# Attention values' high and low parts in one 128-column matrix, padded decay products, and a planner with another matmul time

## The chip, the cores and the metric

The kernel runs on one core of a Trainium2 chip. The metric is the device time of one execution in microseconds (us); the median of three runs stands for it. Below, TensorE (PE) is the matrix engine, VectorE (DVE), ScalarE (ACT) and GpSimd (POOL) the elementwise engines, and SyncE (SP) issues most transfers. PSUM is the memory that products are accumulated in (8 banks of 512 columns here), which VectorE and ScalarE read in this kernel and GpSimd does not.

## The reference

Two model blocks run over 512 tokens of width 1024, in float32.

The first block has a short-convolution layer with a gated feed-forward layer, then an attention layer with three branches (compressed blocks, selected blocks, sliding window) over 16 heads of 64 in 4 groups that share keys and values, again with a feed-forward layer. With 512 tokens all eight selected blocks of 64 fit in the 16 that may be selected, and the window covers the whole sequence, so both branches see every earlier token:

```python
p = jax.nn.softmax(s.reshape(s.shape[:4] + (n_sel * L_SLC,)), axis=-1).reshape(s.shape)
o_slc = jnp.einsum("bghqnl,bgqnld->bqghd", p.astype(v_sel.dtype), v_sel)
...
p = jax.nn.softmax(jnp.where(m, s, NEG_INF), axis=-1)
o_win = jnp.einsum("bghqk,bkgd->bqghd", p.astype(vw.dtype), vw)
o = (gblk[..., 0:1] * o_cmp + gblk[..., 1:2] * o_slc + gblk[..., 2:3] * o_win)
```

The second block has two mixers side by side, a state-space mixer of 16 heads in chunks of 128 tokens, whose weights within a chunk are `decay = exp(where(causal, seg, -inf))`, and a stick-breaking attention of 16 heads, `outs.append(jnp.einsum("bhqk,bhkd->bhqd", weights, vp))`; then an output projection and a feed-forward layer, each scaled by a condition.

## The kernel before

Products in float32 are made of parts: an operand is split into a high part, rounded to the matrix engine's one-pass format, and the low rest (`split`, `hilo`: the high part by a copy, the low one by a subtraction). `mm3` (line 608) issues three products into one PSUM tile: high by high, high by low, low by high. Nearly every product of the kernel comes in such threes; a weight matrix arrives by transfer as `raw`, and is split into `wh` and `wl`.

The activations are held with features on the partitions and the 512 tokens as columns. Stages follow one another: layer a, a feed-forward layer, the keys and values (`nsa`, line 862), attention in 16 units (4 groups times 4 tiles of 128 queries), the output projection "o", a feed-forward layer, the second block's mixers (`block2`, line 1163), and its last layers. `weave` (line 87) interleaves the generators of a stage by fractions of their length, so projections, scores and values of different units stand side by side in the program.

Attention values, first block (`nsa_values`, line 1123): for every key tile and branch (steps: 2, 4, 6 or 8 per unit, 80 in all) four transposes write one PSUM tile "pt"; it is split into "pth" (a copy on ScalarE) and "ptl" (a subtraction on VectorE); three steps later `mm3` multiplies them with the values of that tile, 64 columns of "vh" or "vl", into 64 partitions of one PSUM tile "o". Twelve small products with the compressed values follow, and four copies of 64x128 take "o" to SBUF ("o2"). After the fourth unit of a group both tiles "o2" are split for the output projection.

Values, second block (`sb_out`, line 1559): per head, four key tiles with 512, 384, 256 and 128 query columns, each one `mm3` with 64-column values ("svh", "svl") into 64 partitions of "so", then one copy of 64x512. The values themselves come from `sb_qk` (line 1438) token-major and are split whole, 512 columns at a time.

Decay (`ssd_pair`, line 1354, function `weights`): per head one product "al" spreads a row of the 64-row tile "at" over all partitions, with a selector of 64 rows, `er`, as its matrix; the four "dec" subtractions read it.

The order of the instructions is planned, not written: `Recorder` (line 156) records every instruction, then `arrange` runs a list scheduler forward and backward over durations that `cost` (line 242) gives, and emits each engine's instructions in the planned order. Each engine executes its own in that order. Some instructions may go to one of several engines (`any`, line 195): copies to ScalarE or VectorE, and to GpSimd where both operands are in SBUF on the same partitions and have 256 columns or more; additions and subtractions to VectorE, or GpSimd under the same condition. An addition that reads PSUM has only VectorE. A product's cost is `size * passes / 2.4 + 3.0` ns (line 254), and the next may not start before its own matrix is loaded, columns / 1.2 ns (line 256). The scheduler considers instructions up to 800 places ahead of the first one that is not yet placed.

The lines of almost all instructions are one line of a helper (485), so the profile is read by tile names.

Of the kernel before, what the change touches and what calls it, by code (L numbers as in the profile page):

```python
# [6 lines left out]
F32R = mybir.dt.float32r  # L7
# [4 lines left out]
D = 1024  # L12
# [16 lines left out]
LAG = 3  # L29
# [57 lines left out]
def weave(*streams):  # L87
    """emits instruction streams side by side: (generator, the total of what it yields, start, end)"""
    live = [[float(st[2] if len(st) > 2 else 0), i, st] for i, st in enumerate(streams)]
    while live:  # L90
        s = min(live)
        g, total = s[2][:2]
        a, b = s[2][2:] if len(s[2]) > 2 else (0.0, 1.0)
        try:
            s[0] += (b - a) * next(g) / total
        except StopIteration:
            live.remove(s)
# [12 lines left out]
class View:  # L110
    """an access pattern of a tile that gets its place when the instructions are ordered"""
# [21 lines left out]
class Slot:  # L133
    """one tile as the program sees it, from its first access to its last"""
# [21 lines left out]
class Recorder:  # L156
    """records the instructions of the program, orders those of every engine by the time at which their
    operands are there and by their place in the program, and gives the tiles their places"""
# [8 lines left out]
    # from the end on one engine to the start on another  # L167
# [27 lines left out]
    def any(self, *ways):  # L195
        """one instruction that several engines can do, the usual one first: (engine, method, arguments)"""
# [45 lines left out]
    def cost(self, o, method, a, k, outs, ins):  # L242
        """nanoseconds on the engine, and those of a transfer"""
# [3 lines left out]
        # a scalar per partition  # L247
# [4 lines left out]
        elif o.eng == "tensor":  # L252
            passes = 1 if ins[-1].dtype == F32R else 2 if method == "transpose" else 6
            o.dur = size(outs[0]) * passes / 2.4 + 3.0
            # the next product waits until its own matrix is loaded
            o.load = (int(ins[0].ap.shape[-1]) if method == "matmul" else 128) / 1.2
# [13 lines left out]
    def place(self, ap):  # L270
        """the pattern on the place its tile got"""
# [23 lines left out]
    def backward(self):  # L295
        """the latest starts, from the end of the program"""
# [30 lines left out]
    def forward(self, urgent, look, timed=False):  # L327
# [26 lines left out]
        def avail(t):  # L354
            """when the tile can have a place, or None"""
# [15 lines left out]
        def begin(e, i, limit):  # L371
            """when the engine can start the instruction, or None if not by the limit"""
# [14 lines left out]
            if e in other:  # L387
                # one engine at a time reads a bank
                for t in o.banks:
                    at = max(at, t.read.get(other[e], -1e9) + self.LAG[other[e]][e])  # L390
            if e != o.eng:
                # another engine has to be done with it earlier than the usual one
# [8 lines left out]
        while first < len(ops):  # L401
            best = None
            for e, lst in cand.items():
# [10 lines left out]
                if top is not None and timed and e in self.PATIENT:  # L414
                    # a more urgent one that is ready soon goes first if that makes the later of the two less late
# [74 lines left out]
class Body:  # L490
# [26 lines left out]
    def alike(*views):  # L517
        """whether the Pool engine can do it: in SBUF, on the same partitions, of a size that is worth it"""
# [22 lines left out]
    def copy(self, out, a, scale=None):  # L541
        """a, by a factor"""
# [21 lines left out]
    def load(self, g, parts=None):  # L564
        """starts the transfer of a group of weight blocks"""
# [59 lines left out]
    def dense_g(self, name, n, x, ks=None, m=128):  # L625
        """the same as dense, in steps"""
# [7 lines left out]
    def dense_seq(self, specs, x, ks=None, first=2, late=1):  # L634
        """yields the finished PSUM tile of every (name, n); the late operands are used last in the first tiles,
        or every operand in all of them before the next one"""
# [10 lines left out]
    def dense_halves(self, specs, x, ks=None):  # L647
        """the same for the halves of the tokens, the first halves of all tiles before the second ones"""
# [12 lines left out]
    def dense_late(self, specs, x, first):  # L661
        """dense_seq where the second halves of the tokens come later: the first tiles take them last"""
        out = [self.ps("d") for _ in range(first)]
        for h, sl in enumerate(HALVES):
            for (name, n), p in zip(specs, out):
                # one accumulation group per bank: its first write clears the bank's flags
# [6 lines left out]
    def rsq(self, src, scale, eps):  # L673
        """rsqrt(scale * src + eps) by logarithm and exponential, and a step of Newton"""
# [10 lines left out]
    def allsum(self, acc):  # L685
        """the sums over the partitions, on all of them"""
# [35 lines left out]
    def setup(self):  # L722
# [18 lines left out]
        self.er = self.nc.tile([64, 16], F32R, "er")  # L741
        nc.vector.tensor_copy(self.er, self.cst[0:64, C_E:C_E + 16])
# [71 lines left out]
    def ffn(self, x, rinv, name, gate, after, ada=False, early=0, late=0):  # L814
        """early: the first tiles take the second halves of the tokens last; late: the last tiles in halves"""
# [34 lines left out]
    def dense_out(self, name, x, late, ks=None, **kw):  # L850
        """the tiles of a product with the residual's rows, the last ones in halves: (n, PSUM, columns)"""
# [10 lines left out]
    def nsa(self):  # L862
# [19 lines left out]
        def project():  # L882
            for br, n in (("s", 4), ("w", 8), ("s", 6), ("w", 10)):
                for t in range(2):
# [5 lines left out]
                    else:  # L890
                        self.vt[br, t] = self.hilo(self.transpose4(r), name="v")
# [10 lines left out]
        # gates token-major  # L902
# [50 lines left out]
    def stack(self, r, par, name="qs"):  # L953
        """[hi; lo] of one half of the rows, hi in its own rows"""
# [63 lines left out]
    def nsa_group(self, g):  # L1018
        """operands of one group of heads: stacked queries, doubled keys, distances, compressed values"""
# [103 lines left out]
    def nsa_values(self, g, qt):  # L1123
# [14 lines left out]
        for j in range(len(steps) + LAG):  # L1138
# [6 lines left out]
            if j >= LAG:  # L1145
                kt, br = steps[j - LAG]
                c = 128 * kt + 64 * (g % 2)
                v = self.vt[br, g // 2]
                self.mm3(o[0:64], (v[0][:, c:c + 64], v[1][:, c:c + 64]), x.pop(j - LAG), j == LAG, False)
            yield 1  # L1150
        for h in range(4):
            vh, vl = gr["vc"][:, 64 * h:64 * h + 64], gr["vc"][:, 256 + 64 * h:320 + 64 * h]
            self.mm3(o[0:64, h * 128:(h + 1) * 128], (vh, vl), (ph, pl), False, h == 3)
        for h in range(4):
            dst = o2[h // 2][64 * (h % 2):64 * (h % 2) + 64, qt * 128:(qt + 1) * 128]
            self.copy(dst, o[0:64, h * 128:(h + 1) * 128])
# [6 lines left out]
    def block2(self):  # L1163
        nc = self.nc
        self.cols2()
        # final norm of the first block and the first norm of the second
# [541 lines left out]
```

## Time and profile before

| what | value |
|---|---|
| median of three runs | 2162.2 us (2161.71 to 2162.23) |
| the profiled execution, first to last instruction | 2159.8 us |
| TensorE busy | 2117.5 us, 98% |
| VectorE busy | 1386.1 us, 64% |
| ScalarE busy | 941.8 us, 44% |
| GpSimd busy | 425.9 us, 20% |
| share of the chain that ended last | TensorE 86%, VectorE 9%, ScalarE 2%, issue 2%, GpSimd 1% |
| matrix products | 11113 |

The profile is of one execution, and it shows no time for it other than the span; the median of the runs is 2.4 us above that. Busy is the share of time in which an instruction of the engine is shown as running. For TensorE this says little by itself: products overlap, the end of each is modelled, and one of 512 columns is shown as about 0.39 us whatever the distance to the next. Starts are better: the distance between the starts of neighbours is what a product takes. VectorE's and ScalarE's instructions overlap by about a tenth of a microsecond in the same way. Idle time is what no instruction covers, and the engine named behind the arrow is the one whose result ended it.

### The profile page before, as it was taken

The numbers are of one execution on the slowest core, as the hardware profiler recorded it, in microseconds if no ns is written. First come the engines' busy times: TensorE is split into PE (matmuls) and PEld (weight loads), VectorE is DVE, ScalarE is ACT, GpSimd is POOL, SyncE is SP. The second block draws the span as 40 slices with busy tenths as digits, with TensorE's granted clock in tenths as the row PEclk, the third lists the DMA queues.
The fourth block names the chain that finished last, engine by engine and source line by source line (L and its number), as shares of the span: only waits on it lengthen the run. The fifth ranks groups of instructions, "written<-read, shape, count | busy, mean of one in ns | idle before, by whom it ended". The sixth has DMA issues, their size and how long they took to land.

```text
span 2159.8 us, 28829 instructions
## 1 busy us (share of the span) xinstructions
PE 2117.5 (98%) x11113; PEld 1789.1 (83%) x11113; DVE 1386.1 (64%) x2347; ACT 941.8 (44%) x1587; POOL 425.9 (20%) x558
## 2 busy tenths in 40 slices
PE   8999999999999999999999999999999998999999
PEld 7888888888788777888888887989897888888887
DVE  6578754644868996654355598787879867333333
ACT  4233322332335885322222477677667746222221
POOL 1023320211223763000000141221315222000000
PEclk9999999999999999999999999999999999999999
DMA  4245652533332000222222332111121124222222
GB/s 166 98 178 188 212 183 97 175 117 104 104 127 72 1 1 31 97 98 98 98 98 98 117 127 79 59 50 59 59 69 40 40 95 140 98 98 98 98 98 98
DMA packets 60682, 214.04 MB, mean 99 GB/s; under 512 B 7424, under 2 KB 7552, under 8 KB 60544
## 3 DMA queue, kind: packets, MB, share of 16 engines
q1 hardware_dynamic: 52704, 186.50, 24.9%
q0 software_dynamic: 7840, 25.70, 3.5%
q8 instruction: 87, 1.43, 0.3%
q14 instruction: 51, 0.42, 0.1%
HBM read 210.07 MB, written 2.10 MB: 98 GB/s over the span
## 4 chain that ended last, share of the span: by engine, by line
PE 86%; DVE 9%; ACT 2%; issue 2%; POOL 1%; DMA 0%; SPq 0%; DVEq 0%; ACTq 0%; POOLq 0%
PE d L485 71%; PE qk L485 5%; PE bt L485 2%; PE o L485 2%; DVE wl L485 1%; PE so L485 1%; PE pt L485 1%; PE s L485 1%; DVE pr L485 1%; PE lg L485 1%; DVE e L485 1%; DVE ptl L485 1%; ACT wh L485 1%; DVE ss L485 0%; PE chid L485 0%
## 5 line engine op out<-in xcount | busy, mean ns | idle before, releaser
L485 ACT CAST wh<-raw 128x1024 fp32r<-128x1024 f32 (+1 forms) x332 | 347.6, 1048 | 873.1 <-PE d L485 736.8
L485 DVE TENSOR_TENSOR wl<-raw,wh 128x1024 fp32r<-128x1024 f32 (+1 forms) x342 | 424.6, 1242 | 417.3 <-ACT wh L485 414.5
L485 PE MATMUL d<-xh,wh 128*128 128x512 f32 (+1 forms) x1064 | 417.4, 394 | 6.0 <-ACT xh L485 6.0
L485 PE MATMUL d<-xh,wl 128*128 128x512 f32 (+1 forms) x1064 | 416.5, 392 | 1.0 <-DVE wl L485 1.0
L485 PE MATMUL d<-xl,wh 128*128 128x512 f32 x1064 | 416.3, 391 | 0.0
L485 PE MATMUL d<-hb,wh 128*128 128x512 f32 (+1 forms) x1136 | 332.7, 377 | 3.6 <-ACT hb L485 3.3
L485 PEld LDWEIGHTS d<-xh,wh 128*128 128x128 f32 (+1 forms) x1064 | 200.5, 189 | 47.6 <-ACT xh L485 6.0
L485 PEld LDWEIGHTS d<-hb,wh 128*128 128x128 f32 x1136 | 205.5, 190 | 40.1 <-ACT hb L485 3.5
L485 PEld LDWEIGHTS d<-xh,wl 128*128 128x128 f32 (+1 forms) x1064 | 200.3, 188 | 43.7 <-DVE wl L485 1.8
L485 PEld LDWEIGHTS d<-xl,wh 128*128 128x128 f32 x1064 | 200.4, 188 | 41.6 <-issue 0.7
L485 PE MATMUL d<-hb,wl 128*128 128x512 f32 (+2 forms) x568 | 212.3, 376 | 2.5 <-DVE wl L485 2.5
L485 PE MATMUL d<-hidh,wl 128*128 128x512 f32 (+1 forms) x561 | 211.8, 378 | 0.0
L485 PE MATMUL d<-hidh,wh 128*128 128x512 f32 (+1 forms) x561 | 211.5, 377 | 0.0
L485 PE MATMUL d<-hidl,wh 128*128 128x512 f32 (+1 forms) x561 | 211.5, 377 | 0.0
L485 PE MATMUL qk<-wh,hb 128*128 128x256 f32 x768 | 145.0, 288 | 2.1 <-ACT hb L485 1.0
L485 POOL TENSOR_TENSOR acc<-acc,sq 128x512 f32<-128x512 f32 (+1 forms) x24 | 38.2, 1591 | 499.7 <-ACT sq L485 441.9
L485 PEld LDWEIGHTS qk<-wh,hb 128*128 128x128 f32 x768 | 121.8, 193 | 6.5 <-DVE hb L485 1.5
L485 PEld LDWEIGHTS d<-hb,wl 128*128 128x128 f32 (+1 forms) x568 | 107.3, 190 | 22.6 <-DVE wl L485 3.5
L485 PEld LDWEIGHTS d<-hidl,wh 128*128 128x128 f32 x561 | 105.6, 188 | 19.4
L485 PEld LDWEIGHTS d<-hidh,wh 128*128 128x128 f32 x561 | 105.6, 188 | 19.3
L485 PEld LDWEIGHTS d<-hidh,wl 128*128 128x128 f32 x561 | 105.6, 188 | 19.2
L485 PE MATMUL qk<-wl,hb 128*128 128x256 f32 x384 | 109.0, 286 | 1.5 <-DVE wl L485 1.5
(370 smaller groups left out, 3678.5 us busy)
## 6 DMA issues: line engine op xcount, KB each, us to landing
raw<-in_wall_dram SPq DMA_DIRECT2D x345, 512.0 KB, 3.2
ada<-in_wada_dram POOLq DMA_DIRECT2D x96, 256.0 KB, 4.6
res<-in_x_dram SPq DMA_DIRECT2D x8, 256.0 KB, 7.3
out_dram<-res SPq DMA_DIRECT2D x8, 256.0 KB, 2.0
raw<-in_wall_dram SPq DMA_DIRECT2D x2, 256.0 KB, 3.7
cond<-in_c_dram POOLq DMA_DIRECT2D x2, 256.0 KB, 5.3
cst<-in_consts_dram SPq DMA_DIRECT2D x1, 394.5 KB, 7.0
mst<-in_consts_dram SPq DMA_DIRECT2D x1, 320.0 KB, 3.8
```

Source lines behind the costliest of these rows:

```text
L485: r = getattr(getattr(self.real, o.eng), m)(*[self.place(x) for x in a], **{n: self.place(x) for n, x in k.items()})
```

## The change

Three things change together (comments and descriptions that went out with them are left out here).

- `side` lays the high and low parts of the values next to each other, 64 columns each, so that one 128-column matrix holds both. `mm2` then issues two products instead of three: the pair of value parts by the high part and by the low part of the weights. The upper 64 partitions of the PSUM tile hold what the low part of the values adds; `folded` copies them to SBUF, and an addition joins them with the lower 64. In the first block the small products with the compressed values move ahead of the last pair.
- The decay product's tile `at` and its selector `er` get 128 rows instead of 64, the added ones zero.
- The planner's cost of a product is 17/16 of a 2.4 GHz column plus 1 ns, and the load of a matrix 3 ns more.

```diff
+    COLUMN = 17 / 16 / 2.4
...
-            o.dur = size(outs[0]) * passes / 2.4 + 3.0
-            o.load = (int(ins[0].ap.shape[-1]) if method == "matmul" else 128) / 1.2
+            o.dur = size(outs[0]) * passes * self.COLUMN + 1.0
+            o.load = (int(ins[0].ap.shape[-1]) if method == "matmul" else 128) / 1.2 + 3.0
...
+    def side(self, src, name):
+        p = self.pg(F32R, name)
+        v = p.rearrange("p (a h d) -> p a h d", h=2, d=64)
+        self.split(src.rearrange("p (a d) -> p a d", d=64), v[:, :, 0], v[:, :, 1])
+        return p
+    def mm2(self, out, v, x, start, stop):
+        self.nc.tensor.matmul(out, v, x[0], start=start, stop=False)
+        self.nc.tensor.matmul(out, v, x[1], start=False, stop=stop)
+    def folded(self, p):
+        t = self.pg(name="fo")
+        self.copy(t[0:64], p[64:128])
+        return t[0:64]
...
-        self.er = self.nc.tile([64, 16], F32R, "er")
-        nc.vector.tensor_copy(self.er, self.cst[0:64, C_E:C_E + 16])
+        self.er = self.nc.tile([128, 16], F32R, "er")
+        nc.vector.tensor_copy(self.er, self.cst[:, C_E:C_E + 16])
...
-                        self.vt[br, t] = self.hilo(self.transpose4(r), name="v")
+                        p = self.transpose4(r)
+                        self.vt[br, t] = [self.side(p[:, 256 * i:256 * i + 256], "v") for i in range(2)]
...
-                self.mm3(o[0:64], (v[0][:, c:c + 64], v[1][:, c:c + 64]), x.pop(j - LAG), j == LAG, False)
+                c = 256 * (kt % 2) + 128 * (g % 2)
+                v = self.vt[br, g // 2][kt // 2][:, c:c + 128]
+                last = j == len(steps) + LAG - 1
+                if last:
+                    (the twelve products with the compressed values)
+                self.mm2(o, v, x.pop(j - LAG), j == LAG, last)
...
-            self.copy(dst, o[0:64, h * 128:(h + 1) * 128])
+            self.tt(dst, o[0:64, h * 128:(h + 1) * 128], t[:, h * 128:(h + 1) * 128], ADD)
...
-        self.at = self.pg(F32R, "at")[0:64]
+        self.at = self.pg(F32R, "at")
...
-            mm(al, self.er[:, hd:hd + 1].to_broadcast([64, 128]), self.at, start=True, stop=True)
+            mm(al, self.er[:, hd:hd + 1].to_broadcast([128, 128]), self.at, start=True, stop=True)
...
-            self.sv[i] = [self.hilo(x, name="sv") for x in p]
+            self.sv[i] = [self.side(p[t // 2][:, 256 * (t % 2):256 * (t % 2) + 256], "sv") for t in range(4)]
...
-                c = 256 * (kt % 2) + 64 * (hd % 4)
-                self.mm3(out[0:64, 128 * kt:512], [y[:, c:c + 64] for y in self.sv[2 * (hd // 4)][kt // 2]],
+                c = 128 * (hd % 4)
+                self.mm2(out[:, 128 * kt:512], self.sv[2 * (hd // 4)][kt][:, c:c + 128],
                          (hi[:, o:o + n], lo[:, o:o + n]), u == 2, u == 1)
...
-        self.copy(self.y_sb[-1][64 * h:64 * h + 64], out[0:64])
+        self.tt(self.y_sb[-1][64 * h:64 * h + 64], out[0:64], self.folded(out), ADD)
```

## Rows read from the trace of the kernel before

**Rows 1.** The page's busy times: engine, us, share of the span, instructions.

```profile
PE 2117.5 (98%) x11113; PEld 1789.1 (83%) x11113; DVE 1386.1 (64%) x2347; ACT 941.8 (44%) x1587; POOL 425.9 (20%) x558
```

**Rows 2.** Stretches: length, busy us of five engines (instructions), granted clock, DMA share, GB/s.

```profile
690.00:820.00 130.00, 123.92 (x852) 99.72 (x850) 127.55 (x435) 111.60 (x348) 86.33 (x137) 1.00 0.02 6
820.00:840.00 20.00, 20.00 (x139) 15.60 (x139) 15.34 (x41) 13.67 (x37) 9.83 (x16) 1.00 0.00 1
860.00:900.00 40.00, 40.00 (x176) 32.82 (x175) 26.55 (x35) 14.41 (x17) 2.91 (x4) 1.00 0.27 92
1310.00:1640.00 330.00, 327.44 (x2249) 292.27 (x2248) 265.06 (x449) 233.00 (x398) 78.07 (x109) 1.00 0.18 61
1640.00:1680.00 40.00, 35.99 (x222) 31.10 (x221) 35.04 (x52) 29.24 (x50) 20.60 (x24) 0.96 0.12 41
```

**Rows 3.** TensorE's groups: matrix rows*columns, output, count, busy us, mean ns, idle before.

```profile
L485 PE MATMUL o<-pth,vl 128*64 128x512 f32 x80 | 32.3, 404 | 0.0
L485 PE MATMUL so<-w,svl 128*64 128x512 f32 x16 | 6.3, 396 | 0.0
```

**Rows 4.** Order of time, end of attention: start us, us, engine, what.

```profile
840.33 0.39 PE L485 MATMUL o<-ptl,vh 128*64 128x512 f32 x1
840.56 0.39 PE L485 MATMUL o<-pth,vl 128*64 128x512 f32 x1
840.78 0.22 PE L485 MATMUL o<-pch,vcs 128*64 128x128 f32 x1
...
841.50 0.44 PE L485 MATMUL d<-ol,wh 128*128 128x512 f32 x1
```

**Rows 5.** TensorE's groups from 800 to 845 us.

```profile
L485 PE MATMUL o<-pth,vl 128*64 128x512 f32 x27 | 10.6, 393 | 0.0
```

**Rows 6.** Order of time, TensorE alone, second block's mixers.

```profile
1336.66 0.28 PE L485 MATMUL st<-xsh,btokl 128*128 128x128 f32 x1
1336.77 0.27 PE L485 MATMUL st<-xsh,btokh 128*128 128x128 f32 x1
...
1337.50 0.40 PE L485 MATMUL lg<-ql,ks 128*128 128x512 f32 x1
1337.83 0.50 PE L485 MATMUL al<-at,er 64*128 64x512 f32 x1
1338.25 0.50 PE L485 MATMUL d<-hb,wh 128*128 128x512 f32 x1
...
1756.97 0.28 PE L485 MATMUL so<-w,svh 128*64 128x128 f32 x2
1757.09 0.22 PE L485 MATMUL so<-w,svl 128*64 128x128 f32 x1
1757.15 0.28 PE L485 MATMUL so<-w,svh 128*64 128x256 f32 x1
```

**Rows 7.** VectorE's groups from 685 to 845 us: count, busy us, mean ns, idle before.

```profile
L485 DVE TENSOR_TENSOR ptl<-pt,pth 128x512 fp32r<-128x512 f32 x78 | 50.9, 676 | 1.8 <-ACT pth L485 1.7
L485 DVE TENSOR_TENSOR kx<-kr,kx 64x512 fp32r<-64x512 f32 x8 | 7.0, 873 | 0.4 <-PE sc L485 0.2
L485 DVE TENSOR_TENSOR ol<-o,oh 128x512 fp32r<-128x512 f32 x3 | 2.0, 682 | 0.0
L485 DVE COPY o<-o 64x128 f32<-64x128 f32 x5 | 1.4, 278 | 5.3 <-ACT o L485 5.3
```

**Rows 8.** ScalarE's groups of the same stretch.

```profile
L485 ACT COPY o<-o 64x128 f32<-64x128 f32 x59 | 14.4, 256 | 8.4 <-PE o L485 7.3 <-DVE o L485 0.6
```

**Rows 9.** Order of time, VectorE alone, inside attention.

```profile
772.78 0.29 DVE L485 TENSOR_TENSOR pcl<-pct,pch 128x128 fp32r<-128x128 f32 x1 [0.27 <-ACT pch L485]
772.99 0.18 DVE L485 TENSOR_TENSOR pc<-s,cbias 128x32 f32<-128x32 f32 x1
773.08 0.55 DVE L485 CUSTOM_DVE_ANT_0 pr<-s,bias 128x384 f32<-128x384 f32 x1
...
774.51 2.04 DVE L485 TENSOR_TENSOR pc<-pc,nm 128x128 f32<-128x128 f32 x1
```

**Rows 10.** Instructions of tile "so": count, min/median/max ns, first and last start.

```profile
L485 ACT COPY ysb<-so x10: 567/578/581, 1405.1 to 1759.1; 64x512 f32<-64x512 f32 x10
L485 DVE COPY ysb<-so x6: 672/683/684, 1415.1 to 1728.2; 64x512 f32<-64x512 f32 x6
```

More of the change, by code (lines that the diff above doesn't have):

```diff
@@ L1146, in nsa_values @@
                 kt, br = steps[j - LAG]
-                c = 128 * kt + 64 * (g % 2)
-                v = self.vt[br, g // 2]
-                self.mm3(o[0:64], (v[0][:, c:c + 64], v[1][:, c:c + 64]), x.pop(j - LAG), j == LAG, False)
+                c = 256 * (kt % 2) + 128 * (g % 2)
+                v = self.vt[br, g // 2][kt // 2][:, c:c + 128]
+                last = j == len(steps) + LAG - 1
+                if last:
+                    for h in range(4):
+                        vh, vl = gr["vc"][:, 64 * h:64 * h + 64], gr["vc"][:, 256 + 64 * h:320 + 64 * h]
+                        self.mm3(o[0:64, h * 128:(h + 1) * 128], (vh, vl), (ph, pl), False, False)
+                self.mm2(o, v, x.pop(j - LAG), j == LAG, last)
             yield 1
-        for h in range(4):
-            vh, vl = gr["vc"][:, 64 * h:64 * h + 64], gr["vc"][:, 256 + 64 * h:320 + 64 * h]
-            self.mm3(o[0:64, h * 128:(h + 1) * 128], (vh, vl), (ph, pl), False, h == 3)
+        t = self.folded(o)
         for h in range(4):
             dst = o2[h // 2][64 * (h % 2):64 * (h % 2) + 64, qt * 128:(qt + 1) * 128]
-            self.copy(dst, o[0:64, h * 128:(h + 1) * 128])
+            self.tt(dst, o[0:64, h * 128:(h + 1) * 128], t[:, h * 128:(h + 1) * 128], ADD)
         yield 1
```

## The prediction

> **What bounds the kernel now.** I read the busy shares first, then the engines stage by stage, because a share over 2160 us says nothing about a stage of 150, and last the groups and the order of time inside the stages that the change touches. TensorE is busy for 98% of the span [rows 1]. In a dense stretch the reader should see the floor: 176 products in 40 us with TensorE never idle is 0.227 us for one of 512 columns [rows 2]. So TensorE's time is a count of instructions times a spacing, and a removed product is worth its spacing wherever no other engine is just as full.
>
> It is as full in one place. From 690 to 820 us, the first block's attention, VectorE is busy for 127.6 of 130 us while TensorE shows 123.9, a figure that flatters TensorE because a 512-column product is shown as some 0.39 us although the next starts after 0.23 [rows 2, 4]. ScalarE is at 111.6 and GpSimd at 86.3. So there VectorE sets the pace. From 820 to 840 us it is the other way round: TensorE 20.0 of 20, VectorE 15.3. In the second block's mixers, 1310 to 1640 us, TensorE shows 327.4 of 330 us and VectorE 265.1, 80%: TensorE is the bound. Only a short stretch such as 1640 to 1680 has VectorE at 88% and TensorE waiting (36.0 of 40) [rows 2].
>
> **The change part by part.** The profiled execution spans 2159.8 us; the median of the timed runs is 2162.2, so 2.4 us lie around the span. I take differences from the trace and set them against 2162.2.
>
> *Values of the first block.* There are 80 steps, each with three 512-column products [rows 3]; one of three goes. They start 0.23 us apart although their matrix has 64 columns [rows 4], so width gives nothing back: 80 x 0.23 = 18.4 us of TensorE. The twelve small products with the compressed values stay, ahead of the last pair instead of behind it; TensorE does the same work, so I cost that at nothing.
>
> What replaces the saving is VectorE's. Today 59 of 64 copies out of PSUM run on ScalarE and 5 on VectorE [rows 7, 8]. Afterwards 16 copies of 64x512 (either engine) and 64 additions of 64x128 that read PSUM, which only VectorE can take. No such addition is in the trace. The nearest row is the 128x128 subtraction from PSUM, which is shown as 0.29 us and lets the next instruction start 0.21 us later; a 32-column one lets it start after 0.09 [rows 9]. These are my bounds, 0.09 and 0.29; I take 0.2, by the row of the same column count: 64 x 0.2 = 12.8, less 5 x 0.2 for today's copies there, is +12 us on the engine that is full (bounds +5 to +17). ScalarE gets about 2 us lighter (59 x 0.16 against 16 x 0.48, its shown times less the 0.1 by which neighbours overlap).
>
> What can leave VectorE: three subtractions "ol" and some of the eight "kx" [rows 7], which GpSimd can do too where the partitions match; GpSimd has 44 us free in 130 [rows 2]. I count 4 us (0 to 7). At the end TensorE is the bound: 27 of the 80 steps lie after 800 us [rows 5], about 14 of them, the last two units, after VectorE's saturated stretch; 14 x 0.23 = 3.2 us, and with some earlier ones that had piled up by then I count 4. The fold lengthens the way from the last product to the output projection: a copy (0.58, [rows 10]) and an addition in place of a copy; what hides it is the first two output tiles, which begin with the six older operands; uncovered it costs 0.8 us. Sum for this stage: +12 - 4 - 4 + 0 = **+4 us**, where a count of TensorE alone would say -18. Bounds: -18 (VectorE is not what holds it) to +17.
>
> *Values of the second block.* Per head three products each of 512, 384, 256 and 128 columns become two. The first three are spaced by their columns, 0.23, 0.17 and 0.12 [rows 2]; the last start 0.06 apart [rows 6]. The 128-column ones do not gain: their matrix has 64 columns now, and products of their size with a 128-column matrix in the same mixers start 0.11 apart [rows 6]. Two at 0.11 for three at 0.06 is -0.04. Per head 0.23 + 0.17 + 0.12 - 0.04 = 0.48, times 16 = 7.7 us. In return 16 additions of 64x512 from PSUM on VectorE, near the 0.68 of "ptl" [rows 7], while 6 of the 16 copies there today [rows 10] can go to ScalarE: +6 to +10 us over the 400 us of a stage where VectorE has 20% free. I cost it at 1 us, for the crowded stretches; without cover it is 10.
>
> *Decay products.* The 64-row product starts 0.33 us after a 512-column one and the next follows 0.42 us later, where two neighbours need 0.23 each [rows 6]. If 128 rows make it ordinary, 0.10 + 0.19 = 0.29 goes, times 16 (one for each head) = 4.7 us; the lower bound is 0, that the time belongs to the product itself. The Trainium skill has both readings. TensorE: Matmul & The Clock Gate, section "Why this matters for your kernels", says that a product with few rows takes the same time as one with 128, by which padding would give 0. TensorEngine Tiling (Array Packing), section Key Properties, says that a change of tiling mode drains TensorE, by which the gap on both sides goes. By the first rule the sum is 4.7 less; the gap on either side of the row speaks for the second.
>
> *Values laid side by side.* The same elements are converted in halves: 12 more casts and 12 more subtractions than today's. Half-size forms of each are not shown; from 512 to 128 columns the subtraction from PSUM falls from 0.68 to 0.29 [rows 7, 9], so a split costs 0.15 at most, 1.8 us on each engine, 0 where hidden. The projections beside them are bound by TensorE; I take 0.
>
> *The planner's cost of a product.* 512 columns go from 216.3 to 227.7 ns, beside the 227 of [rows 2]. No product gets faster by it, but the written order of every engine changes, also where nothing else does. In dense stretches, with TensorE full, the order cannot matter. Exposed to it are the 42 us in which TensorE is idle (2159.8 less 2117.5, [rows 1]), outside such stretches. No row gives it a sign; I take 0, bounds -6 to +8.
>
> TensorE's saving in the second block is 7.7 + 4.7 = 12.4. With waits of its own there (36.0 busy of 40 in the crowded stretch) not all arrives: 11.6, less the 1 for VectorE, is -10.6. With +4: **2162.2 - 10.6 + 4 = 2155.6 us**. Should attention leave TensorE idle more, a lower granted clock there costs nothing as long as VectorE is the pace; it is 1.00 now, and 0.96 where TensorE waits most [rows 2].
>
> **The rivals.**
> *Attention follows TensorE after all.* VectorE's 98% holds slow passages: a subtraction of 128 columns, 0.29 us next to it, is once shown as 2.04 [rows 9]. If another order removes these, VectorE has the 12 us free, and 10 to 18 of the 18.4 arrive: 2162.2 - 10.6 - 14 = 2138. Against it: the largest group, 50.9 us of subtractions from PSUM, waited 1.8 us in all [rows 7].
>
> *The new order gives back what the products saved.* Waits of 5 to 8 us appear in the mixers or at the seams between stages; or the padding gives nothing (by the row that would be 2160). Time 2158 to 2166, middle 2161. For it: the 42 us of idle TensorE exist, and any order moves them. Against: the costs come nearer to the trace.
>
> *VectorE takes over attention whole.* Place: 690 to 830 us. Price: the 64 additions at 0.27 instead of 0.2 (+16), nothing moves to GpSimd, the fold is seen at the stage's end (+1). With -10.6 elsewhere: 2169. It decides the sign from the point where attention grows by more than 10.6 us, and a measurable loss from 15. For it: VectorE is full for 130 us without a break. Against: the end of the stage is TensorE's, which gives back.
>
> **How the numbers follow.** The forecast has 0.48 (own range 2149 to 2161), attention with TensorE 0.20 (2130 to 2148), the order 0.20 (2158 to 2166), VectorE whole 0.12 (2166 to 2175). About 0.2%, 4.3 us, is what a measurement of this kernel tells from no change. Faster, below 2157.9: three quarters of the first and all of the second, 0.57. Slower, above 2166.5: the last and a little of the third, 0.14. The same: 0.29. The range 2140 to 2167 leaves out the faster half of the second case and most of the last.
>
> **What would show it.** Counts: 80 products fewer at "o", 64 fewer at "so". "al" followed after 0.23 us and begun 0.23 after its neighbour. 128-column "so" products 0.11 apart. In attention VectorE still 95% busy or more, TensorE's share clearly lower, and the stage's end at 841 to 850 us of the span where it is 841.5 now [rows 4]. If the first "d" of the output projection starts before 832 us, my reading of VectorE as the bound is wrong; if attention is 4 us longer or shorter than that and the whole is still near 2155, the sum was right by luck.

## The result, and the profile after

The changed kernel takes 2197.9 us (median; 2195.98 to 2198.68) where the kernel before, run beside it, takes 2161.95: a ratio of 1.0166, 95% interval 1.0152 to 1.0181. It is slower by 36 us. I had forecast 2155.6, with 2140 to 2167 as the range; the prediction was wrong in sign and size. The profiled execution spans 2196.4 us, 36.6 more than before, and the growth lies in two stages. I cut the span at the down projections of the feed-forward layers (the products "d" from "hid"): a stage runs from the last of one layer to the first of the next, so the products that lead up to "hid" count to the stage ahead of them.

| stage, us | before | after | forecast |
|---|---|---|---|
| up to the end of the first feed-forward layer | 543.2 | 544.3 | 0 |
| keys, values, attention and its output projection | 462.2 | 479.1 | +4 |
| second feed-forward layer | 241.4 | 241.4 | 0 |
| second block's mixers | 669.6 | 688.3 | -10.6 |
| the rest | 243 | 243 | 0 |

The page's busy times after, as [rows 1]:

```profile
PE 2121.7 (97%) x10969; PEld 1791.1 (82%) x10969; DVE 1434.1 (65%) x2434; ACT 945.2 (43%) x1550; POOL 433.9 (20%) x564
```

The 144 products are gone, and TensorE's busy time has not fallen. Its products' shown times, added up, fell by 29.5 us (3929.6 to 3900.1), but products that stand further apart overlap less, and together they cover as much time as before. At "o" they are also shown longer, 0.42 to 0.44 us instead of 0.40, at a granted clock that is 0.97 there. VectorE has 48 us more, 18 of them in attention and 16 in the mixers. The chain that ended last, by engine, of the kernel after (TensorE had 86% and VectorE 9% before):

```profile
PE 80%; DVE 12%; ACT 4%; issue 2%; POOL 1%; DMA 0%; SPq 0%; DVEq 0%; POOLq 0%; ACTq 0%
```

Stretches of the kernel after, columns as in [rows 2]. The last two lie 20 us later than those of before, since the stages do.

```profile
690.00:820.00 130.00, 112.87 (x723) 91.72 (x722) 124.12 (x429) 99.88 (x285) 81.44 (x125) 0.97 0.01 5
820.00:860.00 40.00, 35.34 (x217) 27.35 (x217) 36.51 (x115) 27.65 (x68) 14.12 (x24) 0.96 0.01 1
...
1330.00:1660.00 330.00, 319.90 (x2149) 287.66 (x2147) 263.96 (x445) 224.70 (x380) 81.90 (x110) 0.98 0.17 58
1660.00:1700.00 40.00, 37.19 (x227) 31.54 (x226) 35.93 (x62) 34.85 (x61) 16.16 (x21) 1.00 0.12 41
```

In attention VectorE stands at 124.1 of 130 us and TensorE has dropped from 123.9 to 112.9: the engine that was full has nearly stayed so, at 95%, and the other one waits for it. The stretch from 820 to 860 is new: it was TensorE's from 820 on, now VectorE has 91% of it. In the mixers TensorE is no longer full (327.4 of 330 before, 319.9 now), though VectorE is at the same 80%.

VectorE's groups from 545 to 1030 us of the kernel after: count, busy us, mean ns, idle before.

```profile
L486 DVE TENSOR_TENSOR ptl<-pt,pth 128x512 fp32r<-128x512 f32 x80 | 52.9, 678 | 1.6 <-ACT pth L486 1.3
L486 DVE TENSOR_TENSOR o<-o,fo 64x128 f32<-64x128 f32 x64 | 17.9, 281 | 3.9 <-ACT fo L486 3.1
L486 DVE TENSOR_TENSOR kx<-kr,kx 64x512 fp32r<-64x512 f32 x10 | 7.7, 769 | 0.2
L486 DVE TENSOR_TENSOR ol<-o,oh 128x512 fp32r<-128x512 f32 x6 | 4.4, 750 | 0.0
```

The 64 additions cost 17.9 us of a full engine, less 1.4 for the five copies of [rows 7]. What had been counted on to leave VectorE did not, on balance: over the same stage before it had 12 of these "kx" (9.7 us) and 3 "ol" (2.0), now 10 and 6. Two spacings show in order of time (VectorE, inside attention):

```profile
764.92 0.58 DVE L486 TENSOR_TENSOR o<-o,fo 64x128 f32<-64x128 f32 x2
765.53 0.29 DVE L486 TENSOR_TENSOR pcl<-pct,pch 128x128 fp32r<-128x128 f32 x1
...
770.24 0.27 DVE L486 TENSOR_TENSOR o<-o,fo 64x128 f32<-64x128 f32 x1
770.44 0.67 DVE L486 TENSOR_TENSOR ptl<-pt,pth 128x512 fp32r<-128x512 f32 x1
```

The addition at 770.24 lets the next start after 0.20 us, as I had assumed; the two at 764.92, taken together, take 0.61, so about 0.30 each. The median over all 64 is 0.30.

End of attention, TensorE, kernel after, as [rows 4]:

```profile
858.69 0.22 PE L486 MATMUL o<-pch,vcs 128*64 128x128 f32 x1
858.75 0.44 PE L486 MATMUL o<-pth,v 128*128 128x512 f32 x1
859.03 0.39 PE L486 MATMUL o<-ptl,v 128*128 128x512 f32 x1
859.27 0.39 PE L486 MATMUL d<-oh,wh 128*128 128x512 f32 x1
```

The last product with the values starts at 859.0; before it was about 841.4, just ahead of the 841.50 of [rows 4]. I had given 841 to 850.

### The profile page after: what moved, and what is told of

The parts are those of the page before. It is cut to its first block, busy times and chain, and to the rows that moved or that the text cites. A ratio compares the mean times of both kernels' runs of the same rounds, so it can differ in the third digit from the quotient of the medians.

```text
span 2196.4 us, 28632 instructions
## 1 busy us (share of the span) xinstructions
PE 2121.7 (97%) x10969; PEld 1791.1 (82%) x10969; DVE 1434.1 (65%) x2434; ACT 945.2 (43%) x1550; POOL 433.9 (20%) x564
## 4 chain that ended last, share of the span: by engine, by line
PE 80%; DVE 12%; ACT 4%; issue 2%; POOL 1%; DMA 0%; SPq 0%; DVEq 0%; POOLq 0%; ACTq 0%
PE d L486 69%; PE qk L486 4%; PE bt L486 2%; DVE wl L486 1%; DVE pr L486 1%; PE o L486 1%; DVE ptl L486 1%; PE s L486 1%; PE pt L486 1%; ACT pth L486 1%; ACT wh L486 1%; ACT le L486 1%; DVE rv L486 1%; DVE e L486 1%; ACT pr L486 0%
## 5 line engine op out<-in xcount | busy, mean ns | idle before, releaser
L486 DVE TENSOR_TENSOR wl<-raw,wh 128x1024 fp32r<-128x1024 f32 (+1 forms) x342 | 449.7, 1315 | 418.6 <-ACT wh L486 417.5
L486 ACT CAST wh<-raw 128x1024 fp32r<-128x1024 f32 (+1 forms) x338 | 353.8, 1047 | 847.2 <-PE d L486 719.9
L486 PE MATMUL d<-xh,wh 128*128 128x512 f32 x1064 | 416.3, 392 | 5.8 <-ACT xh L486 5.8
L486 PE MATMUL d<-hb,wh 128*128 128x512 f32 (+2 forms) x1136 | 332.9, 377 | 4.6 <-ACT hb L486 4.0
L486 PEld LDWEIGHTS d<-xh,wh 128*128 128x128 f32 x1064 | 200.1, 188 | 47.8 <-ACT xh L486 5.8
L486 PEld LDWEIGHTS d<-hb,wh 128*128 128x128 f32 (+1 forms) x1136 | 204.9, 190 | 40.9 <-ACT hb L486 4.2
L486 POOL TENSOR_TENSOR acc<-acc,sq 128x512 f32<-128x512 f32 (+1 forms) x21 | 32.5, 1546 | 487.6 <-ACT sq L486 464.7
```

The lines of the kernel that those rows point to most:

```text
L486: r = getattr(getattr(self.real, o.eng), m)(*[self.place(x) for x in a], **{n: self.place(x) for n, x in k.items()})
```

## The experiments

Every kernel ran with the kernel before beside it on the same chip. The ratio's 95% interval is 0.001 to 0.0016 either way, 2 to 3.5 us. "us" is the ratio less one, times 2162. The stages are those of the table above, as differences from before, and come from one profiled execution of each kernel: they need not add up to "us", and the first stage, whose work no edit touches, differs by up to 1.6 us among them.

| run | what it has | us | attention | mixers |
|---|---|---|---|---|
| e1 | the new cost alone | +14.5 | +8.6 | +5.6 |
| e2 | first block's values alone | +17.5 | +17.4 | +0.7 |
| e3 | second block's values alone | +10.2 | -1.7 | +11.5 |
| e4 | padding alone | -5.2 | +0.5 | -5.0 |
| e5 | both values, no fold | +0.4 | -4.6 | +5.9 |
| e6 | whole change but the cost; changed work weighed as before | +24.6 | +11.6 | +9.5 |
| e8 | whole change, old cost | +25.5 | +11.6 | +10.2 |
| e7 | before, 3.1 ns for 3.0 | +6.3 | +1.1 | +3.8 |
| e11 | before, 2.9 ns for 3.0 | +2.2 | +4.2 | -3.1 |
| e9 | order of before, second block's values, no fold | +0.2 | -0.5 | -1.3 |
| e13 | as e9, 64-column matrix | -4.5 | -0.6 | -4.6 |
| e10 | as e9 with the fold | +7.4 | -0.6 | +8.1 |
| e12 | e10 and the padding | +2.4 | +0.1 | +3.7 |
| e14 | order of before, first block's values, no fold | -3.5 | -4.8 | -0.5 |
| e15 | as e14 with the fold | +24.2 | +23.0 | +1.2 |
| e16 | e4, GpSimd's casts on ScalarE | +4.1 | +2.9 | 0.0 |

**One part at a time.** e1 to e4 each have one part of the diff shown ahead:

```diff
+    COLUMN = 17 / 16 / 2.4                                    # e1: the cost and the load
+                self.mm2(o, v, x.pop(j - LAG), j == LAG, last)  # e2: nsa_values, its side() and fold
+                self.mm2(out[:, 128 * kt:512], ...               # e3: sb_out, its side() and fold
+        self.at = self.pg(F32R, "at")                           # e4: at and er with 128 rows
```

> The kernel before with the planner's new cost of a product and nothing else. Theory V (VectorE's added additions make the loss): nothing is added to any engine, so 2158 to 2166 us. Theory O (the planner's new order makes the loss, in the second block above all): some 15 to 25 us slower, 2177 to 2187, with the extra waits between 1250 and 1830 us of the span.

> The kernel before with the attention values of the first block alone laid side by side (two products, a fold), old cost of a product. Theory V: 64 additions of 0.27 us on a VectorE that is full, 12 to 18 us slower, 2174 to 2180, the output projection's first product at 853 to 860 us in place of 836 to 841. Theory O: attention within 5 us of before, 2157 to 2167.

> The kernel before with the values of the second block alone laid side by side, old cost of a product. Theory V: VectorE has room there, so most of the 7.7 us of products arrives: 2154 to 2160. Theory O: the same, since the planner's cost is the old one; a loss here of over 5 us would speak for a third cause, the fold's longer hold of a PSUM tile or the order that the changed program gets.

> The kernel before with the decay products padded to 128 rows and nothing else. Both theories: 3 to 5 us faster, 2157 to 2159, the product followed after 0.23 us in place of 0.42. If the 0.29 us per product belonged to it whatever its rows, 2162.

Measured 2176.0, 2178.9, 2171.3 and 2156.3 us beside some 2161.3. e1 came out just below theory O's range, and more of its loss lies in attention than in the second block, where that theory had it; e2 came out as theory V had it; e3 missed the range of both theories, by a loss of over 5 us that its expectation leaves to a third cause. Three of four parts lose, and the four add up to +37.0 where the whole lost 35.9. The agreement is in the total only: by stages the parts give +25 and +13, the whole +17 and +19, so what a part costs in one order doesn't simply carry over to another.

Padding did what was forecast. "al" in the padded kernel, TensorE, which [rows 6] has with 0.33 ahead and 0.42 behind:

```profile
1338.73 0.40 PE L485 MATMUL lg<-ql,ks 128*128 128x512 f32 x1
1338.97 0.39 PE L485 MATMUL al<-at,er 128*128 128x512 f32 x1
1339.20 0.62 PE L485 MATMUL d<-hb,wh 128*128 128x512 f32 x2
```

0.24 ahead and 0.23 behind. At 2156.3 us, ratio 0.9976 (0.9967 to 0.9986), this kernel is faster than both kernels of the comparison. Of the other runs only e13 and e14 are level with it within the intervals, and they leave a part of the result out.

**Is it the fold?** e5 leaves it out in both blocks and copies the lower 64 partitions as before; neither padding nor the new cost is in it. The cut shows the first block, against the changed kernel.

```diff
-        t = self.folded(o)
...
-            self.tt(dst, o[0:64, h * 128:(h + 1) * 128], t[:, h * 128:(h + 1) * 128], ADD)
+            self.copy(dst, o[0:64, h * 128:(h + 1) * 128])
```

> Both value products laid side by side, old cost, no padding, and the fold left out: the lower 64 partitions alone are copied as before, so what the low parts of the values add is missing from the output. Theory V (the fold's additions on VectorE cost the time): without them products are saved and nothing is added, attention (from the second feed-forward part's end to the next feed-forward's start, 462 us before, 480 with the fold) falls to 448 to 460, the second block's mixers (670 before, 681 with the fold) to 660 to 665; 2142 to 2157 us. Theory O (any changed program gets another order, and that costs): the mixers stay at 675 or more, 2165 to 2175.

2162.56, +0.4. So the 144 products that are gone are worth next to nothing here even where no addition pays for them: attention gains 4.6 of 18.4 us, and the mixers lose 5.9. Theory V has attention right (457.6 us), theory O the mixers (675.5), and neither has the total.

**Is it the order?** e6 and e8 have the whole change but the planner's cost; e6 also has the planner weigh the changed products, casts and additions so that their costs come near those of before. e7 and e11 change nothing but 0.1 ns of the planner's cost, so that it reorders the same instructions. The first two lines are against the changed kernel, the last one replaces that line of the kernel before.

```diff
-            o.dur = size(outs[0]) * passes * self.COLUMN + 1.0
+            o.dur = size(outs[0]) * passes / 2.4 + 3.0          # e6, e8
+            o.dur = size(outs[0]) * passes / 2.4 + 3.1          # e7 (2.9 in e11)
```

> The whole change without the new cost, and with the planner told the durations of before for what was changed: a product of the pair counts 1.5 times, the fold's copy as today's copies, its additions as nothing, the halves as halves of a whole. The order then stays near that of before. Theory V: the additions still run on VectorE, attention 474 to 480, and the mixers get their 12 us of products less up to 10 of additions, 657 to 668: 2160 to 2175 us. Theory O: attention 460 to 468, mixers 657 to 662: 2147 to 2157.

> The changed kernel with the planner's old cost of a product. The single effects add up to 17.7 + 10.0 - 5.0: 2184 us, if they add. Theory O: the new cost is what spoils it, 2165 to 2180. Theory V: 2182 to 2198, attention at 477 to 482 us with either cost.

> The kernel before with 3.1 ns in place of 3.0 in the planner's cost of a product: the same instructions in another order. Theory V: within 4 us of before, 2157 to 2166. Theory O: 5 to 15 us slower, 2167 to 2177, since any new order waits more.

> The kernel before with 2.9 ns in place of 3.0 in the planner's cost of a product: the same instructions in one more order. Theory O (the order of before is a good one among its neighbours): 4 to 12 us slower, 2165 to 2173. If orders scatter to both sides: 2155 to 2168.

2186.4, 2187.4, 2168.0 and 2163.5. The new cost is worth 10.4 us inside the change (1.0166 less 1.0118) and 14.5 alone; the two arbitrary shuffles of the same program cost 6.3 and 2.2 (interval 0.2 to 4.1). e7 is in theory O's range, e11 below it; e6 lies above both of its ranges; e8 is in theory V's, though its attention, 473.8 us, is shorter than the 477 to 482 named there. e6 did not keep the order: 31 of the casts and subtractions that write "w" are on GpSimd there, 18 before. In e1, whose work is the same as before, the attention stretch reads:

```profile
690.00:820.00 130.00, 120.88 (x817) 97.09 (x816) 124.90 (x424) 105.75 (x325) 78.54 (x123) 1.00 0.02 6
```

VectorE has 124.9 where it had 127.6, with 424 instructions instead of 435: it waits more, on a stage in which it is the bound. Nine "o" copies run on it instead of five. That the order costs this is shown; why a cost nearer to the traced spacing gives a worse order is not.

**The order held fixed.** The next runs plan the kernel before, unchanged, and swap instructions only as they are issued: the first two products of three become the pair, the third is left out, and where the fold is in, the copy becomes a copy and an addition (with one fixed place for "fo").

```diff
+                a, b, c3 = self.nc.ops[-3:]
+                a.alt, b.alt, c3.alt = first, second, lambda _: []   # e9, e13: sb_out; e14: nsa_values
...
+            return [(o.eng, "copy" if o.eng == "scalar" else "tensor_copy", (f, out[64:128]), {}),
+                    ("vector", "tensor_tensor", (y, out[0:64], f, ADD), {})]   # e10, e12; e15 alike
```

> The kernel before with its own order, instruction by instruction: only in the second block's values each three products become the two with the 128-column matrix, and each split of the values is issued as two halves in its place. The fold is left out, so what the low parts of these values add is missing. Theory O (the products' saving is real, and it was the new order that ate it in the runs before): the mixers shrink from 670 to 661 to 664 us, 2153 to 2157. Theory W (TensorE does not bound the mixers, so removed products are worth little there whatever the order): 668 to 671, 2159 to 2163.

> The same with the fold: behind each head's last product its copy takes the upper half to SBUF on the engine that copied before, and an addition on VectorE follows at once. The difference to the run without it is the price of 16 additions of 0.6 us. Theory V: 5 to 10 us, 2159 to 2166. Theory O: hidden, 0 to 3 us more, 2153 to 2159.

> Padding and the second block's merged products with their fold, all in the order of before: a candidate for the fastest. Padding gives 5.0 as before; with theory O 2149 to 2154, with theory V or W 2155 to 2161.

> As e9 (order of before, block-2 values in two products instead of three, no fold, low part of the values left out), but each product takes only the 64 columns of the high part as its matrix. Nothing else differs. Theory 'wide load': in e9 the products 'so' between short ones paid some 55 ns each for a 128-column load, 64 products of each of two kinds; with 64 columns they start 0.23, 0.17, 0.12 and 0.06 after each other, the neighbours 'lg' of 128 columns return from 6.6 to 3.4 us, and 5 to 9 us come back: 2153 to 2157, the 7.7 that I had forecast. Rival 'another engine bounds the mixers': nothing comes back, 2160 to 2163, and TensorE idles more.

e9 took 2161.8 us, +0.2: 7.7 us of products, as I had counted them, are gone from the stage that TensorE bounds, and nothing arrives. e10 took 2169.7: the fold alone costs 7 by the ratios, 9 in the mixers of the profiled executions. e12, 2164.3, takes 5.0 off that by the padding, which therefore adds to the rest without loss. e13 took 2158.0, 4.8 us less than e9 by the ratios (4.0 by the spans). e9 is in the range of theory W; e10 and e12 lie above all of theirs; e13 is 1 us above that of the wide load and 2 below that of its rival. The same place in order of time, TensorE, first e9 and then e13:

```profile
1548.15 0.22 PE L486 MATMUL lg<-qh,ks 128*128 128x128 f32 x1
1548.21 0.45 PE L486 MATMUL so<-w,svh 128*128 128x512 f32 x1
1548.49 0.23 PE L486 MATMUL lg<-ql,ks 128*128 128x128 f32 x1
1548.56 0.44 PE L486 MATMUL so<-w,svh 128*128 128x512 f32 x1
```

```profile
1546.71 0.22 PE L486 MATMUL lg<-qh,ks 128*128 128x128 f32 x1
1546.77 0.40 PE L486 MATMUL so<-w,svh 128*64 128x512 f32 x1
1547.00 0.22 PE L486 MATMUL lg<-ql,ks 128*128 128x128 f32 x1
1547.06 0.40 PE L486 MATMUL so<-w,svh 128*64 128x512 f32 x1
```

With a 128-column matrix the 512-column product lets the next start after 0.28 us, with a 64-column one after 0.23. Over the mixers the median spacing of the four sizes is 0.286, 0.228, 0.171 and 0.112 in e9, and 0.231, 0.176, 0.118 and 0.060 in e13 and before: some 55 ns on every one, whatever its size. The loads themselves are shown as 0.188 us (e9) and 0.134 (e13), 54 ns apart. The Trainium skill, TensorE: Matmul & The Clock Gate, section "LDWEIGHTS (loading the stationary operand)", says that a load takes its columns divided by 1.2, in ns. By that page an estimate is 107 for 128 columns and 53 for 64; the 54 between them agrees with the 55 measured.

The 55 shows only behind a short product, as at most places of this order. In e3, a 512-column "so" lets the next start after 0.286 us (median of 5) where the product before it has 128 columns, and after 0.228 (of 15) where that has 512; in the kernel after it is 0.285 (of 4) and 0.228 (of 17). e3 was ordered with the wide load known to the planner, and its "so" mostly stand behind long products: the medians are 0.232, 0.176, 0.118 and 0.108 there, and 0.231, 0.175, 0.119 and 0.108 in the kernel after.

The other half of what e9 misses is waiting: a product removed ahead of a wait only lengthens the wait. TensorE in the kernel before, and the same place in e9:

```profile
1650.71 0.22 PE L485 MATMUL lg<-ql,ks 128*128 128x128 f32 x1
1650.77 0.40 PE L485 MATMUL so<-w,svl 128*64 128x512 f32 x1
1653.26 0.50 PE L485 MATMUL bt<-qh,ks 128*128 128x512 f32 x1 [2.09 <-DVE ks L485]
```

```profile
1651.82 0.23 PE L486 MATMUL lg<-ql,ks 128*128 128x128 f32 x1
1654.32 0.80 PE L486 MATMUL bt<-qh,ks 128*128 128x512 f32 x1 [2.27 <-DVE ks L486]
```

From "lg" to "bt" it is 2.55 us before and 2.50 in e9, with a product of 0.23 less. Over the mixers "so" takes 31.6 us of TensorE's time before, 25.7 in e9 and 20.2 in e13, 2.5 of the difference being this one wait that now stands behind an "lg"; the stage is 4.6 shorter in e13. One thing in the expectation was wrong: the growth of the 128-column "lg" is that wait and not a load, and it stayed (6.6 us in e9, 7.1 in e13).

**Attention with the order fixed.**

> Order of before; in attention the three products of a step become two with a 128-column matrix, the small products with the compressed values come ahead of the last pair, and the fold is left out (the low part of the values is missing from the result). 80 products, 18.4 us of TensorE, fewer. Theory 'VectorE sets the pace of attention': 3 to 6 us come back, at the end of the stage, 2156 to 2159. Rival 'attention follows TensorE': 12 to 18 come back, 2144 to 2150. If VectorE is the pace and the order alone had cost e5 something, the gain is somewhat over the 4.6 that the stage showed there.

> As e14, with the fold: per unit one copy of 64x512 and four additions of 64x128 on VectorE in place of four copies (59 of 64 of these ran on ScalarE). Theory 'the fold is the loss, at 0.28 us an addition on a full VectorE': 64 x 0.28 less 5 x 0.2 = 17 us above e14, 2172 to 2177. My forecast's price of 0.2 would give 2168 to 2171. Rival 'the re-planned order is the loss' (e2 was 2178.9): at most 5 above e14, 2158 to 2163.

e14 took 2158.5 us, -3.5; e15 2187.0, +24.2. The stretch of 690 to 820 us, in e14 and then in e15:

```profile
690.00:820.00 130.00, 119.85 (x803) 98.38 (x801) 128.53 (x446) 112.76 (x352) 89.12 (x140) 1.00 0.02 5
```

```profile
690.00:820.00 130.00, 107.41 (x684) 87.84 (x682) 121.75 (x412) 93.06 (x262) 77.61 (x123) 0.95 0.02 5
```

e14 is the clean test of the bound: TensorE is relieved of 80 products in attention, little else changes (the splits of the values come in halves, the last pair behind the small products), and VectorE is at 128.5 of 130 while 4.2 us come back at the end. The last product with the values:

```profile
837.28 0.39 PE L486 MATMUL o<-ptl,vl 128*128 128x512 f32 x1
```

Of the two readings VectorE's is right. That the wide load ate the saving here too is ruled out: from each large "o" product to the next start it is 60.6 us in all before and 43.8 in e14, so 16.8 of the 18.4 did leave TensorE. With the fold in the old order VectorE idles as well. VectorE's group and the waits of TensorE in e15:

```profile
L493 DVE TENSOR_TENSOR o<-o,fo 64x128 f32<-64x128 f32 x64 | 17.5, 281 | 9.9 <-ACT fo L493 8.4 <-PE o L493 0.7
```

```profile
PE pct L493 <- DVE pc L493: 6.7, 7, 1.8
PE sc L493 <- DVE pc L493: 4.8, 3, 2.0
...
PE s L493 <- DVE nm L493: 3.3, 6, 0.8
```

The additions stand where the copies stood, VectorE waits 8.4 us there for ScalarE's copy of the upper half, and what is queued behind them ("pc", "nm") makes TensorE wait. A part is e15's own: with one place for "fo", ScalarE's copies wait 3.3 us for additions, which they do not in the kernel after. The expectation had 2172 to 2177 and missed this. The planner, in e2, placed the additions better (+17.5), so the re-planned order saves part of the fold's price there; it doesn't cause the whole of it.

**GpSimd beside VectorE.** In e3 and e5 the planner put 29 and 30 of the casts and subtractions that write "w" on GpSimd instead of 18. A place in e3, GpSimd, VectorE and TensorE in turn:

```profile
1512.48 2.39 POOL L485 TENSOR_TENSOR wl<-raw,wh 128x1024 fp32r<-128x1024 f32 x1
```

```profile
1512.83 2.60 DVE L485 SCALAR_TENSOR_TENSOR rv<-ry,rv 128x512 f32<-128x512 f32 x1
1515.46 0.69 DVE L485 TENSOR_TENSOR rv<-rv,ry 128x512 f32<-128x512 f32 x1
```

```profile
1518.84 1.22 PE L485 MATMUL d<-ysh,wh 128*128 128x512 f32 x2 [3.04 <-ACT ysh L485]
```

A VectorE instruction that takes at most 0.69 us in the kernel before takes 2.60 and ends 0.56 us after GpSimd's subtraction does; TensorE waits soon after. e16 takes every cast from GpSimd that ScalarE can do:

```diff
+            if eng == "gpsimd" and "scalar" in o.ways:
+                eng, (m, a, k) = "scalar", o.ways["scalar"][1]
```

> The padded kernel e4, its order kept, with every cast that the plan gives to GpSimd issued by ScalarE at the same place. Theory 'GpSimd beside VectorE stretches VectorE's instructions, and the mixers wait for that': VectorE's busy time falls by 5 us or more, and the kernel is 1 to 4 us faster than e4's 2156, 2152 to 2155. Rival 'the stretch is hidden, and ScalarE now is late': VectorE's busy time falls all the same, and the kernel is 2156 to 2165.

VectorE's busy time fell by 8.8 us (1377.0 against 1385.8 in e4), and the kernel took 2166.0, 9.3 us more than e4. The rival was right, at 1 us above its range: VectorE's instructions are shorter without GpSimd's casts, but at these places that is hidden, and ScalarE is not the engine to give the casts to ("d" waits 1.8 us for its "ysh", "qk" 2.0 for "we" in the mixers). GpSimd's subtractions, as in the place above, stayed where they were, so what they cost in e3 and e5 is not tested.

## Why the prediction was wrong, point by point

Attention missed its forecast by 12.9 us, the mixers by 29.3. Three steps carry that: the price of the additions on a full VectorE, the saving in the mixers that was taken as arriving with a fold at 1 us, and, with about 15 us the largest, the planner's order, which was put at nothing.

**What bounds each stage** held for VectorE in attention (e14), and in part for TensorE in the mixers: the padding's 5.0 us arrived whole, but of the 8.9 us of "so" products that left in e13 only 4.6.

**Values of the first block** failed in three of its terms. The forecast had "64 x 0.2 = 12.8", "I count 4 us" for what moves to GpSimd, and 4 for TensorE's tail: +4 in all. The additions take 0.28 to 0.30 each; nothing net left VectorE, whose shown times in the stage add up to 409.0 us where it was 390.7, +18.3; and the tail's gain, 4.2 us in e14 where there is no fold, was covered by it, as VectorE stayed full to the end. The stage grew by 16.9. That is the case "VectorE takes over attention whole", priced at +17 and given 0.12. That the two numbers agree so closely is in part luck: the same work on VectorE, planned with the old cost, makes the stage 11.6 us longer (e8), and in the old order 23.0 (e15). The upper bound of 0.29 was the right price: an addition that reads PSUM and SBUF has the row of the 128x128 subtraction as its nearest, and I took its spacing at one place (0.21) for its price at all.

**Values of the second block**: the sum "Per head 0.23 + 0.17 + 0.12 - 0.04 = 0.48" held in the changed kernel, whose "so" products are spaced as it says. Without the waits of over 1 us they take 20.8 us of TensorE's time, 29.1 before: 8.3 are gone, 7.7 were forecast. The step that failed is that they would arrive ("11.6" of 12.4). In e5, which has no fold, 9.2 are gone in the same way, and the mixers are 5.9 us longer. In the order of before, where "so" stands behind short products, the sum itself fails too: the wide load costs 55 ns on all four sizes, 4.0 us by e13, and the rest of the 7.7 went into waits for other engines; e9 is 0.2 slower. "I cost it at 1 us" for the 16 additions was wrong as well: 7 us (e10), inside my own bound of "+6 to +10". VectorE at 80% of a stage was no cover; I had read a share as a place to hide. Which chain brings the 7 is not shown: TensorE idles 26.3 us in the mixers of e10 and 21.5 in e9, and the largest new wait, 2.2 us of "y" for "mh", is for ScalarE.

**Decay products**: 4.7 forecast, 5.0 measured. By the rule of the Trainium skill that was weighed there first (TensorE: Matmul & The Clock Gate, section "Why this matters for your kernels"), that a product with few rows takes the same time as one with 128, nothing would have come; the row decided.

**Values laid side by side**: taken as 0; no run has it alone, so it stays inside e5 and e9, which are at +0.4 and +0.2 in all.

**The planner's cost of a product**: taken as 0 with bounds of -6 to +8. It costs 14.5 alone and 10.4 in the change, beyond the bounds. "In dense stretches, with TensorE full, the order cannot matter" was the fault: attention is dense on VectorE, and the order there decides both how often VectorE waits and which engine gets a copy (e1). In the mixers the order is most of the loss. e12 has all of their changed work in the order of before, and they are 3.7 us longer; planned anew with the old cost they are 10.2 longer (e8), with the new cost 18.7. So 3.7 is the work, and 15 the order. The rival "The new order gives back what the products saved" had this mechanism, with waits of 5 to 8 us where 15 came. Both shuffles that mean nothing were slower, by 2.2 and 6.3 us; two are too few to say that the order of before is better than all its neighbours, but a change that makes the planner plan again should be priced with several us either way, not at zero.

**What stays open**: what the lower granted clock of attention costs (0.97 now); no run separates it from the waits. And why the new orders wait more: that they do is shown (TensorE idles 36.1 us in the mixers after, 28.3 in e12, 21.3 before), by which choice of the planner is not. No run has the changed program in an order as good for it as the old one is for the kernel before.

The waits that hold TensorE in the mixers after, longest first, show no single one to blame:

```profile
PE d L486 <- ACT hb L486: 4.0, 1, 4.0
PE ssp L486 <- DVE acc L486: 3.7, 2, 3.0
PE d L486 <- DVE wl L486: 3.5, 3, 1.9
PE qk L486 <- DVE le L486: 2.5, 3, 1.2
```

## What to carry to other kernels

Price a removed product by the engine that is full in its stage, and price what replaces it at the long end if it lands there: 18.4 us less on TensorE returned 3.5, and 64 small additions took it back several times over. When a stationary matrix gets wider, count the longer load on every product that stands behind a short one, whatever its own length. Where a planner orders the program, test each edit with the order held fixed too; a new plan of the same instructions moved this kernel by up to 14.5 us (e1).

## What the runs showed of the hardware

- A 128-column matrix costs 55 ns more than a 64-column one on a product behind one of 128 columns, up to products of 512 columns (0.286 against 0.231 us, e9 and e13), and next to nothing behind one of 512 (0.228, e3).
- A VectorE instruction with both operands in SBUF was stretched from 0.69 to 2.60 us beside a GpSimd subtraction of 2.39 us (e3). The Trainium skill, SBUF — State Buffer, section "Who interferes with whom", says that a VectorE instruction with two SBUF inputs contends with a GpSimd instruction that reads SBUF; the trace agrees. The additions that read one operand from PSUM were not stretched: 18 of the 64 of the kernel after run wholly inside a GpSimd instruction, and the longest takes 286 ns where the mean of all is 281.
- A product with 64 rows among such with 128 cost 0.31 us more than a padded one (5.0 us over 16).
